# Empty slices in the projection schedule of a stick-breaking attention layer, a later split of the turned values, and a lead-in stepped at every second slot

## The chip, the cores and the metric

The kernel runs on one core of a Trainium2 chip. A core has a matmul engine (TensorE, PE in the profile; its weight loads are PEld), three engines for elementwise work (VectorE or DVE, ScalarE or ACT, GpSimd or POOL) and SyncE (SP), which here issues the DMAs. Each engine works through its own list of instructions in order, and semaphores make one wait for another. Matmul results land in PSUM, which has eight banks of 128 x 512 numbers; everything else lies in SBUF or in device memory.

The metric is the time of one execution on the device, in microseconds (us): the median over several.

## The reference

One layer of a transformer with 2048 tokens of width 1024: a norm, stick-breaking attention with 16 heads of 64, an output projection with residual, another norm, and a gated feed-forward part (width 2816). The part that matters here, for each block of 128 queries (h is the normed and modulated input):

```python
qkv = (h @ w_qkv).reshape(b, s, 3, N_HEADS, HEAD_DIM)
z = jnp.einsum('bthd,bshd->bhts', q[:, q0:end], k[:, :end]).astype(jnp.float32) * scale
mask = s_pos < t_pos
sp = jnp.where(mask, jax.nn.softplus(z), 0.0)
rest = lax.cumsum(sp, axis=3, reverse=True)
log_a = jnp.where(mask, z - rest, -jnp.inf)
a = jnp.exp(log_a).astype(v.dtype)
outs.append(jnp.einsum('bhts,bshd->bthd', a, v[:, :end]))
...
return o @ w_o
```

The kernel uses that a weight is sigmoid(z) times the product of sigmoid(-z) over the later keys, so each row needs two sigmoids, one running product (a scan) and one multiplication.

## The kernel before

All matrix products are made from numbers split in a high and a low half: high times high, high times low, low times high. Each operand therefore needs a split first, a copy that rounds (ScalarE) and a subtraction (VectorE or GpSimd).

**Units and slots.** Heads are handled in 8 pairs, tokens in 4 blocks of 512. A unit is one head, one block of queries and one block of keys; there are 160. A unit takes four slots, one for each 128 queries, so the attention stage has 640 slots, and the loop at lines 1067 to 1099 writes out, slot by slot, what each engine is to do: the scheduler is switched off for the four compute engines (line 165), and what is written first runs first on its engine. SP isn't among them; its DMAs are ordered by the framework.

A slot runs stages of several units at once (`ORDER_IN_SLOT`, lines 57 to 61). Of slot s: `score` (two matmuls into `z`), `sigmoids` (ScalarE twice), `break_sticks` (the scan on VectorE, then a multiplication on GpSimd); of the weights made six slots before: `turn` (four 128 x 128 transposes into a PSUM tile `t`, two turns in every even slot), `split_high` (ScalarE's copy) and `split_low` (VectorE's subtraction) into `aT`; of nine slots before: `weigh_values` (two matmuls into the accumulator `o`). In even slots the turns stand behind the projection and ahead of the sigmoids and splits.

**Projections between.** Between `score` and `turn` stands `proj`: a part of the projections of queries, keys and values, which are computed block by block as the attention goes on (`project`, lines 376 to 483). For each of 32 steps (a head pair and a token block) it makes three products, keys, queries, values, each in 8 slices of three matmuls (`mm3`), into a tile `pj`. Behind the keys and behind the queries `split` copies the result out of PSUM, and DMAs move it to its place. The values are copied to `vT`; `VGAP` = 2 empty slices later `values_turn` transposes them into PSUM (`vt`, four transposes) and splits them (lines 463 to 476). `project` is a generator: each `yield` ends a slice, and `project_to` (line 500) advances it to a given count of slices. `SLICES` says how many slices each step has, `AHEAD` how many must be done at the start, and `RATE` spreads the rest evenly over the slots (a slot on the diagonal counts 0.8). The first two steps are done differently (`early`): their values are turned within the next steps.

**PSUM.** Three pools hold the eight banks: `zps` 3 (`z`), `tps` 2 (`t`), `accps` 3. The last is shared by `pj`, `vt`, `o`, some of the turned inputs `xT`, and the sums `ap` of the modulation, which other generators (`late`, line 1073) put between the slots.

**The end of the stage.** When all slices are done, at slot 608, `first_out`, the output projection of the first token block, is begun; from 28 slots before the end of the units on it makes one slice in each slot. Its inputs, the attention's outputs, are loaded, added (GpSimd) and split by `lead_in` (lines 967 to 976), inputs 6 and 7 by a second call of it. That generator is stepped from line 1077 in every third slot and from line 1087.

The rest of the kernel (output projection, norm, feed-forward) is the same before and after.

Of the kernel before, what the change touches and what calls it, by code (L numbers as in the profile page):

```python
# [19 lines left out]
KC = D // P  # L20
NH = 16
HD = 64
NPAIR = NH // 2
BT = 512
NB = S // BT
# [11 lines left out]

VGAP = 2

SLICES = [0, 3 * KC] + [3 * KC + VGAP] * (NPAIR * NB - 2)  # L40


AHEAD = 6 * KC + 6
DIAG_WEIGHT = 0.8
RATE = (sum(SLICES) - AHEAD) / (NPAIR * (48 + 32 * DIAG_WEIGHT) - 24 - 8 * DIAG_WEIGHT)

# [40 lines left out]
def hybrid_trunk_kernel(  # L87
# [83 lines left out]
    def sb(shape, dtype, **kw):  # L171

        return (odd if kw["tag"] in ODD_TAGS else att).tile(shape, dtype, **kw)
# [5 lines left out]
    def load_weights(p, t, tag="wraw"):  # L179
        raw = sb([P, KC, P], F32, name=f"wr{p}_{t}", tag=tag, bufs=BUFS[tag])  # L180
        nc.sync.dma_start(raw, wqkv[p, t])
        raws[p, t] = raw
# [152 lines left out]
    def h_load(p, b):  # L335
        h = []
        for k2 in range(KC // 2):
            ht = sb([P, 2, 2, BT], F32R, name=f"ht{p}_{b}_{k2}", tag="ht", bufs=BUFS["ht"])
            nc.sync.dma_start(f32(ht), h_s[b][:, 2 * k2 : 2 * k2 + 2])
            h += [ht[:, 0], ht[:, 1]]  # L340
        return h
# [14 lines left out]
    waiting = []  # L356
# [19 lines left out]
    def project(at):  # L376

        p, b = STEPS[at]
        begun = (p, b) == (0, 0)
        early, parked = (p, b) in EARLY, (p, b) == PARKED  # L380

        nb = STEPS[at + 1][1] if at + 1 < len(STEPS) and STEPS[at + 1][0] == 0 else None
        if STEPS[at] == (PARKED[0], 1):
            unpark()
        h = norm_h[b] if p == 0 or parked else h_load(p, b)

        def product(t):
            if begun:
                return first_acc[t]
            w = weights[p, t]  # L390
            if parked and t == 1:
                acc = zps.tile([P, BT], F32, name=f"pj{p}_{b}_{t}", tag="z")
            else:
                acc = accps.tile([P, BT], F32, name=f"pj{p}_{b}_{t}", tag="acc")
            ahead = b == NB - 1 and p + 1 < NPAIR
            for k in range(KC):
                if t == 1:
                    if p == 0:
                        first_norm(b, k + 3)
                    if k == 0 and nb and nb > 1:  # L400
                        x_load(nb)
                    if k == 5 and waiting:
                        waiting.pop()()
                if parked and t == 1 and k % 2 == 0:
                    nc.sync.dma_start(*stores[k // 2])
                if parked and (t, k) == (1, 6):
                    split_early(1, 2, ["whl"])
                if t == 0 and nb:
                    (x_square if k < 4 else x_scale)(nb, k % 4)
                if t == 2 and k in (2, 4, 6):  # L410
                    first_norm(nb, k // 2 - 1)
                if ahead and k == 0:
                    load_weights(p + 1, t)
                if ahead and k == 6:
                    split_weights(p + 1, t)
                mm3(acc, (w[0][:, k], w[1][:, k]), (h[k][:, 0], h[k][:, 1]), k == 0, k == KC - 1)
                yield
            return acc

        def split(acc, tag):  # L420
            hl = sb([P, 2, BT], F32R, name=f"{tag}n{p}_{b}", tag="qkn", bufs=BUFS["qkn"])
            nc.scalar.copy(hl[:, 0], acc)
            nc.vector.tensor_tensor(hl[:, 1], acc, f32(hl[:, 0]), op=ALU.subtract)
            return hl

        closing = (p, b) == (NPAIR - 1, NB - 1)
        if closing:
            wo_load(0, 0, "whl")
            wo_load(0, 1, "ht")
        n = split((yield from product(1)), "k")  # L430
        if closing:
            wo_load(0, 2, "whl")
        if parked:
            nc.sync.dma_start(k_park, f32(n))
        else:
            kt = sb([P, 2, BT], F32R, name=f"kt{p}_{b}", tag="kt", bufs=BUFS["kt"])
            for e in range(2):
                for part in range(2):
                    nc.sync.dma_start(
                        f32(kt[part * HD : (part + 1) * HD, e]), f32(n[e * HD : (e + 1) * HD, part])  # L440
                    )
            keys[p, b] = kt

        n = split((yield from product(0)), "q")
        if closing:
            wo_load(0, 3, "whl")
        if parked:
            nc.sync.dma_start(q_park, f32(n))
        else:
            qt = sb([P, 2, 2, BT], F32R, name=f"qt{p}_{b}", tag="qt", bufs=BUFS["qt"])  # L450
            for e in range(2):
                for half in range(2):
                    nc.sync.dma_start(
                        f32(qt[half * HD : (half + 1) * HD, e]), f32(n[e * HD : (e + 1) * HD])
                    )
            queries[p, b] = qt

        acc = yield from product(2)
        tag = "w" if early else "tmp"
        vT = sb([P, BT], F32, name=f"vT{p}_{b}", tag=tag, bufs=BUFS[tag])  # L460
        nc.scalar.copy(vT, acc)

        def values_turn():
            pool, ptag = (zps, "z") if early else (accps, "acc")
            pt = pool.tile([P, 4, 2, HD], F32, name=f"vt{p}_{b}", tag=ptag)
            for i in range(4):
                nc.tensor.transpose(
                    pt[:, i].rearrange("p e d -> p (e d)"), vT[:, i * P : (i + 1) * P], ident
                )
            v = sb([P, 4, 2, 2, HD], F32R, name=f"v{p}_{b}", tag="v", bufs=BUFS["v"])  # L470
            nc.scalar.copy(v[:, :, :, 0], pt)
            nc.vector.tensor_tensor(v[:, :, :, 1], pt, f32(v[:, :, :, 0]), op=ALU.subtract)
            if parked:
                nc.sync.dma_start(v_park, f32(v))
            else:
                values[p, b] = v

        if early:
            waiting.append(values_turn)
            return  # L480
        for _ in range(VGAP):
            yield
        values_turn()

    units = [
        (p, e, qb, sc)
        for p in range(NPAIR)
        for qb in range(NB)
        for e in range(2)
        for sc in range(qb, -1, -1)  # L490
    ]
# [8 lines left out]
    def project_to(n):  # L500

        nonlocal done
        while done < min(n, sum(SLICES)):
            next(pending)
            done += 1
        if done == sum(SLICES):
            next(pending, None)
# [557 lines left out]
    first_out = None  # L1065
    project_to(AHEAD - EAGER)
    for s in range(4 * len(units) + last):
        if s % 4 == 0 and s // 4 < len(units):
            p, e, qb, sc = units[s // 4]
            at = STEPS.index((p, qb)) if (p, qb) != PARKED else STEPS.index((p, 1)) - 1  # L1070
            project_to(sum(SLICES[: at + 1]) + 1)
        if s >= LATE_FROM and s % LATE_STEP == 0:
            next(late, None)
        if s >= SPLIT_FROM and s % SPLIT_STEP == 0:
            next(wo_weights, None)
        if s >= lead_from and s % WO_STEP == 0:
            next(ahead_of_wo, None)
        if done == sum(SLICES):
            if first_out is None:
                first_out = out_projection(0)  # L1080
                for k2, tag in enumerate(("ht", "ht", "ht", "ht")):
                    wo_load(1, k2, tag)
                for step in ahead_of_wo:
                    pass
                ahead_of_wo = lead_in(6, KC)
            elif s < 4 * len(units):
                next(ahead_of_wo, None)
            if s == 4 * len(units):
                gate_load(0, gate)
            if s >= 4 * len(units) - OUT_BEFORE:  # L1090
                for _ in range(1 if s < 4 * len(units) else 3):
                    next(first_out, None)
        for stage, delay in ORDER_IN_SLOT[s % 2]:
            if stage == "proj":
                i = min(s // 4, len(units) - 1)
                weight += DIAG_WEIGHT if units[i][2] == units[i][3] else 1.0
                project_to(AHEAD - max(0, EAGER - 1 - s) + weight * RATE)
            elif 0 <= s - delay < 4 * len(units):
                stages[stage](*divmod(s - delay, 4))
# [501 lines left out]
```

## Time and profile before

| | us |
|---|---|
| median of three runs | 2847.78 |
| lowest and highest | 2846.89, 2852.01 |
| the profiled execution | 2847.31 |
| its span, from the first to the last instruction of the program | 2845.1 |

In the profile, "busy" is the time in which an engine has an instruction running; `x` gives a number of instructions. A row of waits names the engine that stood still, the line and the tile of the instruction that couldn't start, and what it waited for, then the total, the number of waits and the longest. A row of the timeline has the start and the length in us, engine, line, operation, output and inputs, shape, and in brackets how long the engine was idle before and what ended that. Matmuls are pipelined: one of 512 columns is shown with some 0.39 us, but the next starts after 0.23 us; starts tell the pace. The attention stage lies between about 50 and 1390 us.

### The profile page before, as it was taken

To read this page: it belongs to the slowest core of one execution; us is meant where nothing else is said; L and a number is where in the kernel's file an instruction comes from. 1 tells how busy PE (TensorE), PEld (TensorE's weight loads), DVE (VectorE), ACT (ScalarE), POOL (GpSimd) and SP (SyncE) were. 2 spreads that over 40 slices of the span, in tenths; PEclk is the share of its full clock that TensorE was granted. 3 is DMA by queue.
4 is the path that set the end of the run, shared out by engine and by line. 5 is a ranking of instruction groups with operands and counts; after the bars stand their busy time and mean duration, and the time that the engine had idled before them with its cause. 6 is when DMAs were issued, how large, how long until landed. Compare 5 with 4: busy or idle time off the path is not lost.

```text
span 2845.1 us, 41790 instructions
## 1 busy us (share of the span) xinstructions
PE 2795.6 (98%) x13848; PEld 2333.9 (82%) x13848; DVE 2028.4 (71%) x2822; ACT 1632.3 (57%) x3265; POOL 1277.0 (45%) x2032
## 2 busy tenths in 40 slices
PE   7999999999999999999999999999999999999998
PEld 6788888888888888887888888888788888888887
DVE  6788898888888888888866766555775665133467
ACT  5787877788787877777645533333433333322243
POOL 1475666676576655656410122221222222544454
PEclk9999999999999999999999999999999999999999
DMA  8765556656665635546289645435453335545566
GB/s 329 271 211 167 189 155 227 211 170 234 189 209 192 209 118 179 196 133 231 88 299 312 203 137 152 122 98 161 130 177 108 112 107 163 191 142 155 180 214 195
DMA packets 239368, 516.84 MB, mean 182 GB/s; under 512 B 22321, under 2 KB 110385, under 8 KB 221489
## 3 DMA queue, kind: packets, MB, share of 16 engines
q1 hardware_dynamic: 239152, 514.18, 56.0%
q8 instruction: 109, 1.79, 0.3%
q14 instruction: 107, 0.87, 0.1%
HBM read 346.85 MB, written 118.49 MB: 164 GB/s over the span
## 4 chain that ended last, share of the span: by engine, by line
PE 87%; DVE 6%; ACT 2%; DMA 2%; issue 2%; POOL 1%; SPq 0%; DVEq 0%; POOLq 0%; ACTq 0%
PE s L155 9%; PE s L156 9%; PE s L157 9%; PE z L519 8%; PE o L598 8%; PE t L570 8%; PE pj L155 6%; PE pj L156 6%; PE pj L157 6%; PE o L156 4%; PE o L157 4%; PE o L155 4%; PE y L157 2%; PE y L155 2%; PE y L156 2%
## 5 line engine op out<-in xcount | busy, mean ns | idle before, releaser
L560 POOL TENSOR_TENSOR a<-a,w 128x512 f32<-128x512 f32 (+3 forms) x640 | 619.4, 968 | 217.8 <-DVE w L553 126.8
L553 DVE TENSOR_TENSOR_SCAN w<-z,c,begin 128x512 f32<-128x512 f32 x384 | 489.6, 1279 | 81.2 <-ACT z L538 61.5
L155 PE MATMUL s<-r,l 128*128 128x512 f32 x1232 | 481.4, 391 | 4.3 <-DVE p L1364 3.7
L157 PE MATMUL s<-r,l 128*128 128x512 f32 x1232 | 479.4, 389 | 0.0
L156 PE MATMUL s<-r,l 128*128 128x512 f32 x1232 | 479.3, 389 | 0.0
L536 ACT ACTIVATE a<-z 128x512 f32<-128x512 f32 (+3 forms) x640 | 347.2, 543 | 167.2 <-PE z L519 135.7
L598 PE MATMUL o<-aT,v 128*128 128x512 f32 (+3 forms) x1280 | 384.3, 381 | 0.1
L586 DVE TENSOR_TENSOR aT<-t,aT 128x512 fp32r<-128x512 f32 (+3 forms) x640 | 359.3, 596 | 22.9 <-ACT aT L580 22.2
L519 PE MATMUL z<-kt,qt 128*128 128x512 f32 (+3 forms) x1280 | 363.1, 365 | 0.0
L580 ACT CAST aT<-t 128x512 fp32r<-128x512 f32 (+3 forms) x640 | 314.1, 533 | 73.5 <-PE t L570 63.5
L538 ACT ACTIVATE z<-z 128x512 f32<-128x512 f32 (+3 forms) x640 | 344.8, 539 | 0.0
L1372 POOL TENSOR_TENSOR one<-p,p 128x512 f32<-128x512 f32 x44 | 70.5, 1602 | 577.8 <-issue 320.5
L155 PE MATMUL pj<-ht,w 128*128 128x512 f32 x768 | 309.7, 403 | 7.6 <-ACT ht L705 2.6
L156 PE MATMUL pj<-ht,w 128*128 128x512 f32 x768 | 302.0, 393 | 1.2 <-DVE ht L710 0.7
L570 PE MATMUL t<-begin,a 128*128 128x128 f32 x2176 | 294.8, 273 | 8.5 <-DVE aT L586 7.2
L570 PEld LDWEIGHTS t<-begin,a 128*128 128x128 f32 x2176 | 255.1, 140 | 58.0 <-DVE aT L586 10.8
L157 PE MATMUL pj<-ht,w 128*128 128x512 f32 x768 | 302.1, 393 | 0.0
L155 PEld LDWEIGHTS s<-r,l 128*128 128x128 f32 x1232 | 231.3, 188 | 54.4 <-ACT l L1225 2.9
L157 PEld LDWEIGHTS s<-r,l 128*128 128x128 f32 x1232 | 231.3, 188 | 48.2
L156 PEld LDWEIGHTS s<-r,l 128*128 128x128 f32 x1232 | 231.3, 188 | 47.9 <-issue 0.5
L548 DVE TENSOR_TENSOR_SCAN w<-z,begin 128x128 f32<-128x128 f32 (+3 forms) x256 | 208.8, 818 | 75.0 <-ACT z L538 62.2
L519 PEld LDWEIGHTS z<-kt,qt 128*128 128x128 f32 x1280 | 230.3, 188 | 37.4 <-DVE w L548 0.2
(160 smaller groups left out, 4865.8 us busy)
## 6 DMA issues: line engine op xcount, KB each, us to landing
ht<-h_s SPq DMA_DIRECT2D x108, 1024.0 KB, 8.1
wi<-in_win SPq DMA_DIRECT2D x86, 512.0 KB, 4.0
qt<-qn SPq DMA_DIRECT2D x124, 256.0 KB, 4.8
ol_qt<-act_s SPq DMA_DIRECT2D x56, 512.0 KB, 3.7
act_s<-S SPq DMA_DIRECT2D x66, 256.0 KB, 4.1
br<-in_wout SPq DMA_DIRECT2D x66, 256.0 KB, 3.6
h_s<-ht SPq DMA_DIRECT2D x16, 1024.0 KB, 7.8
o_s<-os SPq DMA_DIRECT2D x128, 128.0 KB, 2.4
```

Source lines behind the costliest of these rows:

```text
L155: nc.tensor.matmul(acc, lhs[0], rhs[0], start=first, stop=False, **kw)
L156: nc.tensor.matmul(acc, lhs[0], rhs[1], start=False, stop=False, **kw)
L157: nc.tensor.matmul(acc, lhs[1], rhs[0], start=False, stop=last, **kw)
L519: nc.tensor.matmul(z[:, :n], q[:, e, part, r * P : (r + 1) * P], k[:, e, :n], start=part == 0, stop=part == 1,)
L536: nc.scalar.activation(a[:, :n], z[:, :n], AF.Sigmoid, scale=QK_SCALE)
L538: nc.scalar.activation(z[:, :n], z[:, :n], AF.Sigmoid, scale=-QK_SCALE)
L553: nc.vector.tensor_tensor_scan(rest[:, rev], left[:, rev], begin[:, :BT][:, rev], initial=carries[r], op0=ALU.mult, op1=ALU.bypass,)
L560: nc.gpsimd.tensor_tensor(a[:, :n], a[:, :n], rest[:, 1 : n + 1], op=ALU.mult)
L570: nc.tensor.transpose(pt[:, rb * P : (rb + 1) * P], weighed[i, rb][:, j * P : (j + 1) * P], ident)
L580: nc.scalar.copy(hl[:, 0, t0:], pt[:, t0:])
L586: nc.vector.tensor_tensor(hl[:, 1, t0:], pt[:, t0:], f32(hl[:, 0, t0:]), op=ALU.subtract)
L598: nc.tensor.matmul(acc[:, t0:], lhs, hl[:, part, t0:], start=sc == qb and j == 0 and part == 0, stop=sc == 0 and j == 3 and part == 1,)
```

## The change

A step of the projections now has four more slices: an empty one behind the split of the keys, one behind that of the queries, one between the transposes of the values and their split, and one behind that split. The counts (`SLICES`, `AHEAD`, and `RATE` from them) follow. The two early steps keep their slices. In the end of the stage, the second call of `lead_in` is stepped in even slots where it was stepped in every one. No instruction is added, removed or reshaped.

```diff
 VGAP = 2
-SLICES = [0, 3 * KC] + [3 * KC + VGAP] * (NPAIR * NB - 2)
-AHEAD = 6 * KC + 6
+PAUSES = 4
+SLICES = [0, 3 * KC] + [3 * KC + VGAP + PAUSES] * (NPAIR * NB - 2)
+AHEAD = 6 * KC + 6 + PAUSES
...
         n = split((yield from product(1)), "k")
+        if not early:
+            yield
...
         n = split((yield from product(0)), "q")
+        if not early:
+            yield
...
                 nc.tensor.transpose(
                     pt[:, i].rearrange("p e d -> p (e d)"), vT[:, i * P : (i + 1) * P], ident
                 )
+            return pt
+
+        def values_split(pt):
             v = sb([P, 4, 2, 2, HD], F32R, name=f"v{p}_{b}", tag="v", bufs=BUFS["v"])
             nc.scalar.copy(v[:, :, :, 0], pt)
             nc.vector.tensor_tensor(v[:, :, :, 1], pt, f32(v[:, :, :, 0]), op=ALU.subtract)
...
         if early:
-            waiting.append(values_turn)
+            waiting.append(lambda: values_split(values_turn()))
             return
         for _ in range(VGAP):
             yield
-        values_turn()
+        pt = values_turn()
+        yield
+        values_split(pt)
+        yield
...
-            elif s < 4 * len(units):
+            elif s < 4 * len(units) and s % 2 == 0:
                 next(ahead_of_wo, None)
```

## The prediction

> **What bounds the kernel now.** I read the page first, then busy time by stretch, then who waited for whom, then groups by shape, then the timeline around the longest waits. The page:
>
> ```profile
> span 2845.1 us, 41790 instructions
> PE 2795.6 (98%) x13848; PEld 2333.9 (82%) x13848; DVE 2028.4 (71%) x2822; ACT 1632.3 (57%) x3265; POOL 1277.0 (45%) x2032
> PEclk9999999999999999999999999999999999999999
> ht<-h_s SPq DMA_DIRECT2D x108, 1024.0 KB, 8.1
> ```
>
> PE is busy for 98% of the span at the full clock, so PE's order of work matters only where PE waits. The edit adds, removes and reshapes no instruction; it can move at most the 49.5 us in which PE is idle, or lengthen them. The edit acts in the attention stage. Busy time by stretch (PE, PEld, DVE, ACT, POOL, then clock and DMA):
>
> ```profile
> 200.00:1300.00 1100.00, 1089.93 (x6011) 924.27 (x6010) 943.24 (x1225) 865.54 (x1826) 697.00 (x1450) 1.00 0.58 186
> 1326.00:1336.00 10.00, 8.57 (x56) 7.16 (x56) 8.90 (x12) 7.79 (x18) 6.22 (x14) 1.00 0.97 396
> ```
>
> From 200 to 1300 us PE idles 10.07 us, and VectorE is busy for 86%: not the bound over the stage, but near enough to become it wherever PE's load per slot drops. The second row is such a place already (the last block's projections are over, the output projection not yet begun): PE drops to 86% there, VectorE rises to 89%. The same stretch for the score matmuls alone (PE, PEld) counts the slots, two matmuls each:
>
> ```profile
> 200.00:1300.00 1100.00, 308.08 (x1086) 195.52 (x1086) 1.00 0.58 186
> ```
>
> 1086 / 2 = 543 slots, 2.03 us each. What PE waited for, from 200 to 1300, then from 60 to 200 (three rows), then from 1300 to 1360 (the last row); columns are total, times, longest:
>
> ```profile
> PE t L570 <- DVE aT L586: 3.3, 7, 0.8
> PE pj L155 <- issue: 1.4, 1, 1.4
> PE pj L155 <- DVE qn L423: 1.4, 1, 1.4
> PE pj L155 <- DVE kn L423: 0.9, 1, 0.9
> PE ap L277 <- DVE v L472: 0.7, 1, 0.7
> PE vt L467 <- ACT vT L461: 0.7, 1, 0.7
> PE t L570 <- POOL w L188: 0.6, 1, 0.6
> ...
> PE xT L315 <- DVE qn L423: 1.0, 1, 1.0
> PE t L570 <- DVE aT L586: 1.0, 3, 0.5
> PE pj L155 <- ACT hf L325: 0.9, 1, 0.9
> ...
> PE t L570 <- DVE aT L586: 2.9, 4, 1.2
> ```
>
> Two kinds of wait. A transpose `t` waits for a PSUM buffer that `split_low` on VectorE has not emptied: VectorE is late. A product `pj` (or `xT`) waits for an `accps` buffer that the splits of keys or queries, or a neighbour, still hold: there are three, and PE asks for the next at once.
>
> **The change part by part.**
>
> *Empty slice behind keys and queries.* Now the next product's first matmul stands in the same slice as the split of the one before. Timeline rows of the longest such wait:
>
> ```profile
> 545.55 0.39 PE L157 MATMUL pj<-ht,w 128*128 128x512 f32 x1
> 545.98 0.59 ACT L422 CAST qn<-pj 128x512 fp32r<-128x512 f32 x1 [1.77 <-PE pj L157]
> 546.60 0.69 DVE L423 TENSOR_TENSOR qn<-pj,qn 128x512 fp32r<-128x512 f32 x1 [0.91 <-ACT qn L422]
> 547.35 0.50 PE L155 MATMUL pj<-ht,w 128*128 128x512 f32 x1 [1.40 <-DVE qn L423]
> ```
>
> PE ends the queries at 545.94, ScalarE and VectorE need until 547.29, and PE stands. With an empty slice PE first does a slot's values and scores. Starts of neighbouring 512-wide matmuls, and one pair of turns:
>
> ```profile
> 299.46 1.04 PE L570 MATMUL t<-begin,a 128*128 128x128 f32 x8
> ...
> 301.48 0.39 PE L156 MATMUL pj<-ht,w 128*128 128x512 f32 x1
> 301.71 0.39 PE L157 MATMUL pj<-ht,w 128*128 128x512 f32 x1
> ```
>
> 0.23 us a matmul, so two of values and two of scores are 0.92 us, a slice of projection (three) 0.69 us, and eight transposes, in every second slot, at most 1.04 us: an empty slot is at most 0.92 + 0.52 = 1.44 us of PE work. The empty slice thus covers 0.92 us of a wait: the 0.9 us (`kn`) goes wholly, the 1.4 us (`qn`) leaves 0.5. That is -1.8. The same for `xT<-qn`, before 200 us: -0.9. Bounds: 0, if another buffer is late next (`o`, `ap`, `vt` share the ring), and -3.3, if all three go.
>
> *Empty slice behind the values, split a slice later.* The wait put down to issue is the same kind: VectorE's modulation work before the values' split held the buffer.
>
> ```profile
> 863.89 0.17 DVE L239 SCALAR_TENSOR_TENSOR g_eff<-sc,gc 128x4 f32<-128x4 f32 x1
> 863.96 0.47 PE L155 MATMUL pj<-ht,w 128*128 128x512 f32 x1 [1.42 <-issue]
> ```
>
> The next block's first product now comes one or two slots after the four transposes of the values instead of right behind them: -0.9 of 1.4 (bounds 0 and -1.4). `ap<-v` (0.7) stays: that split isn't earlier. ScalarE no longer meets the transposes still running. VGAP stays 2 slices but slices pass faster, so the transposes may meet ScalarE's copy `vT` a little sooner: 0.7 us once now, once more is 0 to +0.7; I take 0.
>
> *Slices pass faster.* 804 slices become 924 and AHEAD goes from 54 to 58; worked through RATE's own line, 1.34 becomes 1.55 slices for each full slot, about 0.14 us more PE work in a slot between pauses. In the order in which the two built programs' instructions stand, slots 12 to 603 without a projection matmul go from 43 to 96: a block's end had one or two, followed by a slot with the values' transposes and a product; now it has two or three, the transposes among them, and single ones stand behind keys and queries.
>
> *The price.* ScalarE and VectorE work of a full slot, by shape, 200 to 1300 us (busy, mean ns, then idle before):
>
> ```profile
> L553 DVE TENSOR_TENSOR_SCAN w<-z,c,begin 128x512 f32<-128x512 f32 x325 | 414.3, 1279 | 71.5 <-ACT z L538 54.5 <-POOL c L559 6.2 <-POOL w L535 4.0
> L586 DVE TENSOR_TENSOR aT<-t,aT 128x512 fp32r<-128x512 f32 x379 | 244.2, 675 | 10.8 <-ACT aT L580 10.6
> L536 ACT ACTIVATE a<-z 128x512 f32<-128x512 f32 x380 | 230.8, 607 | 97.2 <-PE z L519 83.3 <-POOL a L560 4.4 <-POOL w L535 4.1
> L538 ACT ACTIVATE z<-z 128x512 f32<-128x512 f32 x380 | 229.2, 603 | 0.0
> L580 ACT CAST aT<-t 128x512 fp32r<-128x512 f32 x379 | 211.8, 595 | 48.5 <-PE t L570 47.8
> L472 DVE TENSOR_TENSOR v<-vt,v 128x512 fp32r<-128x512 f32 x26 | 17.6, 677 | 2.7 <-ACT v L471 2.5
> L471 ACT CAST v<-vt 128x512 fp32r<-128x512 f32 x26 | 15.8, 609 | 6.7 <-PE vt L467 6.7
> ```
>
> VectorE needs 1.28 + 0.68 = 1.95 us a slot, ScalarE 1.81, an empty slot of PE 1.44: each falls VectorE 0.5 us behind, and `v` adds 0.68. How this comes to a stop is seen at one block's end (PE, timeline):
>
> ```profile
> 302.84 0.60 PE L570 MATMUL t<-begin,a 128*128 128x128 f32 x4
> 303.99 0.31 PEld L570 LDWEIGHTS t<-begin,a 128*128 128x128 f32 x3 [0.78 <-DVE aT L586]
> ```
>
> Second turn of a pair: it waits for the buffer before last. Bounds of one more empty slot at 29 ends: 0, if the slack covers it all (3.3 us over some 27 ends now is 0.12 each, so most ends have slack to spare), and 29 x 0.5 = +14.5 if none does. I take half of what these waits cost now, +1.7, nearer the lower end: the slots between the pauses carry 0.14 us more each, which lets VectorE catch up, and the 6.7 us for which ScalarE stood before `v` on unfinished transposes go from the chain turn, copy, subtract. Behind keys and queries only one slot is empty, with slack restored: bounds 0 and 58 x 0.5 = +29; I take +0.5, next to the lower one, because slots with one and two slices stand directly on both sides.
>
> *First block's last outputs.* `lead_in(6, KC)` has five steps: load of 6, load of 7, add of 6, add of 7 with the split of 6, split of 7. Two places call it: line 1077 in every third slot, which stays, and line 1087, now in every slot, then in even ones. From slot 608, where both programs see the last slice done, that gives now 609 (both loads), 610, 611, 612, and then 609, 610, 612 (both adds and the split of 6) and 614: the order of POOL's instructions shows the two adds side by side. The split on ScalarE comes right behind its own add instead of a slot later. Already now it has to wait:
>
> ```profile
> 1336.78 0.62 ACT L941 CAST ohl<-of 128x512 fp32r<-128x512 f32 x1 [1.64 <-POOL w L533]
> 1338.94 0.66 PE L570 MATMUL t<-begin,a 128*128 128x128 f32 x4 [1.19 <-DVE aT L586]
> ```
>
> ScalarE stood 1.64 us for POOL, the turned weights' copies behind it in its queue, VectorE's `ohl` subtract behind that, and PE 1.19 us for the subtract after it. With the distance of one slot (2.03 us) gone ScalarE stands up to that much longer; against it, from slot 612 on PE has 0.69 us of output projection in each slot, so it comes later to the turn that waits. Bounds -1.2 (the later place heals it) and +2.0; I take +1.5, nearer the upper one, since POOL's queue in front of the add (multiply 1.1 us, copy) is the same. The halves of 6 are used at slot 618, of 7 at 619, five or six slots behind their splits. The stretch without projections there is one slot longer: +0.5 (0 to +0.5).
>
> *Queues.* SP's order shifts by a place or two of small transfers; POOL's weight splits move by at most a slot. A tile of `ht` lands in 8.1 us (first fence); between its last read and its next lie 10 slices before, 12 now, over 7 slots or some 15 us. Cost nothing; if that cover went, a late tile would cost what 8.1 us exceeds.
>
> *Sum.* -1.8 - 0.9 - 0.9 + 1.5 + 1.7 + 0.5 + 0.5 = +0.6 us. The profiled execution took 2847.31 (span 2845.1 and 2.2 around it), 0.5 under the median of the three runs, 2847.78. 2847.3 + 0.6 = 2847.9: no change.
>
> **The rivals.** 0.2% is 5.7 us, about what a measurement here can tell from no change.
>
> *VectorE becomes the bound at block ends (slower).* Place: the second turn of a pair after the values. For: 1.95 against 1.44 us, and the 8.90 of 10 us in the stretch without projections. Against: most ends have slack. Gains (-3.6) against 14.5 at the ends, a quarter of the 29 behind keys and queries (7) and 2.0 for the lead-in and its longer stretch is +20: 2867; half of the first two gives +9, 2856. Without any price behind keys and queries it decides from 0.25 us an end (29 x 0.25 = 7.3 = 5.7 + 3.6 - 2.0).
>
> *The gaps heal too (faster).* ScalarE no longer stands before `v`, the slices between the pauses are denser, and `t<-aT` goes as well: of the 10.07 us in the stage all but the two 0.7 and the 0.6 (8.1), 2.8 before 200 and 2.9 at the end is -13.8: 2833.5; half is 2840.5.
>
> *Nothing moves but places.* Each wait reappears at another buffer, only the lead-in's 2.0 is added: 2849.3.
>
> *The clock drops.* By the row at 1326, ten microseconds almost without projections ran at 1.00, so the empty slots shouldn't lose it; if one did, 29 gaps of two slots at 1.44 us would double: +84, 2931. [...]
>
> **How the numbers follow.** Forecast, terms that nearly cancel, with "nothing but places" inside the band of no change: 0.50. Gaps heal: 0.26. VectorE bound: 0.23. Clock: 0.01. The range takes the half-effects and a little more, 2838 to 2858; outside are the full rivals and the clock, under 2 in 10. The likeliest case's own range is 2842 to 2853. Faster by over 0.2%: 0.26; within: 0.50; slower: 0.24.
>
> **What would show it.** Right: `pj<-kn`, `pj<-qn`, `xT<-qn` and the 1.4 us of issue gone or under 0.5; ScalarE's idle before `v` near zero; ScalarE before the first `ohl` of 6 idle for over 1.64 us and PE's wait behind it longer than 1.19; `t<-aT` between 3 and 7 us from 200 to 1300. Wrong: `t<-aT` over 10 us (slower), or near zero (faster); a `pj` or `o` that waits for a new holder of `accps`; PEclk under 1.

## The result, and the profile after

The changed kernel takes 2862.56 us (median; 2859.12 to 2868.31) against 2847.98 for the kernel before (2846.89 to 2852.01): ratio 1.0048, 95% interval 1.0038 to 1.0058 (ratios here and below are estimated over all the runs, so they can differ a little from the quotient of the medians, here 1.0051). It is slower by some 14.6 us, where no change was forecast. The profiled execution took 2862.93 us.

The page's lines, then busy time by stretch (PE, PEld, DVE, ACT, POOL, clock, DMA), of the changed kernel:

```profile
span 2861.1 us, 41812 instructions
PE 2804.8 (98%) x13848; PEld 2338.5 (82%) x13848; DVE 2021.7 (71%) x2822; ACT 1627.8 (57%) x3265; POOL 1275.0 (45%) x2032
```

```profile
200.00:1300.00 1100.00, 1085.41 (x5972) 917.50 (x5971) 930.70 (x1216) 853.60 (x1810) 688.22 (x1436) 1.00 0.57 183
```

Each of the five rows of engines has the same number of instructions as before (the page's total of all kinds is 41812, it was 41790). The span is 16.0 us longer. From 200 to 1300 PE idles 14.6 us, it was 10.1, and the window holds 39 matmuls fewer. What PE waited for, from 200 to 1300:

```profile
PE t L582 <- DVE aT L598: 9.3, 22, 0.7
PE pj L157 <- DVE qn L425: 1.8, 2, 1.0
PE pj L157 <- ACT os L616: 1.1, 1, 1.1
PE vt L473 <- ACT vT L467: 0.7, 1, 0.7
PE pj L157 <- DVE kn L425: 0.4, 1, 0.4
PE t L582 <- POOL c L571: 0.4, 1, 0.4
PE pj L157 <- DVE gr L282: 0.2, 1, 0.2
PE t L582 <- POOL a L572: 0.2, 1, 0.2
```

The transposes' waits for VectorE's subtraction went from 3.3 us in 7 places to 9.3 in 22. Their mechanism at one block's end (timeline, rows of PE and VectorE, ScalarE's copies into `aT` and its `v` copy):

```profile
520.80 2.46 DVE L565 TENSOR_TENSOR_SCAN w<-z,c,begin 128x512 f32<-128x512 f32 x2 [0.77 <-ACT z L550]
...
521.29 0.60 PE L473 MATMUL vt<-begin,vT 128*128 128x128 f32 x4
...
521.59 0.62 ACT L592 CAST aT<-t 128x512 fp32r<-128x512 f32 x1
...
522.07 0.63 ACT L480 CAST v<-vt 128x512 fp32r<-128x512 f32 x1
...
522.54 0.64 ACT L592 CAST aT<-t 128x512 fp32r<-128x512 f32 x1
...
523.18 0.67 DVE L598 TENSOR_TENSOR aT<-t,aT 128x512 fp32r<-128x512 f32 x1
...
523.76 0.68 DVE L481 TENSOR_TENSOR v<-vt,v 128x512 fp32r<-128x512 f32 x1
...
523.90 0.66 PE L582 MATMUL t<-begin,a 128*128 128x128 f32 x4 [0.57 <-DVE aT L598]
...
524.36 0.68 DVE L598 TENSOR_TENSOR aT<-t,aT 128x512 fp32r<-128x512 f32 x1
...
525.18 0.63 PE L582 MATMUL t<-begin,a 128*128 128x128 f32 x4 [0.63 <-DVE aT L598]
```

PE has run through slots without a product, so two scans stand in VectorE's queue back to back, then a subtraction, the values' subtraction, another subtraction, with no gap between them. ScalarE's copies for the two subtractions had ended 0.97 and 1.18 us before these began. PE reaches the turns and stands 0.57 us for the first buffer and 0.63 for the second.

A row of waits counts only the gaps that the profile gives to one releaser, and its matmuls overlap: those shown with 0.39 us start 0.23 us apart. The trace's starts tell more. I take the start of each slot's first score matmul as the slot's mark, and call a matmul late by its start-to-start distance from the one before it less the median distance of the same pair of kinds in the kernel before, where that is over 0.06 us. Between the marks of slots 40 and 600 this gives, for the kernel before and after: length 1136.0 and 1143.4 us; transposes `t` late by 7.7 us in 24 places and 15.9 in 42; `pj` late by 7.7 and 4.9. Of the transposes' 7.7 us, 5.7 lie within 6 us behind the values' copy `vT`, at 11 of the stage's 26 block ends; after, 11.0 at 19 of 26. Within 6 us behind the copies of keys and queries lay 0.6, now 2.7.

The starts also show what the late turns waited for. In the changed kernel the first transpose of a turn is late in 40 places between the two marks, 15.4 us in all. Each of them starts 0.05 to 0.15 us after VectorE has ended the subtraction of two turns before, which frees its buffer. In 37 of them (14.4 us) that subtraction had begun over 0.15 us after ScalarE's copy for it was finished, in the median of the 40 places 0.8 us: VectorE was busy with other work all that time. It hadn't always been kept busy before: in some two thirds of the 37 it stood idle for part of the 3 us ahead (0.5 us in the mean of all), as for 0.77 us in the first row above, where it waited for ScalarE's sigmoid. So ScalarE has a part in VectorE's lateness; how large it is wasn't tested.

At the lead-in (timeline, then PE's waits from 1300 to 1370):

```profile
1354.12 0.62 ACT L953 CAST ohl<-of 128x512 fp32r<-128x512 f32 x1 [3.90 <-POOL of L946]
...
1357.79 1.73 PE L582 MATMUL t<-begin,a 128*128 128x128 f32 x7 [3.09 <-DVE aT L598]
```

```profile
PE t L582 <- DVE aT L598: 4.8, 3, 3.1
```

ScalarE waits 3.90 us ahead of the first split of input 6, 1.64 before, and PE 3.09 behind it, 1.19 before.

The changed kernel reaches the mark of slot 639 16.1 us later. This splits into 4.3 up to slot 40, 7.4 from 40 to 600, and 4.4 from 600 on, all by the two profiled executions.

### The profile page after: what moved, and what is told of

Its sections match the earlier page's. It is cut to its first block, busy times and chain, and to the rows that moved or that the text cites. A ratio compares the mean times of both kernels' runs of the same rounds, so it can differ in the third digit from the quotient of the medians.

```text
span 2861.1 us, 41812 instructions
## 1 busy us (share of the span) xinstructions
PE 2804.8 (98%) x13848; PEld 2338.5 (82%) x13848; DVE 2021.7 (71%) x2822; ACT 1627.8 (57%) x3265; POOL 1275.0 (45%) x2032
## 4 chain that ended last, share of the span: by engine, by line
PE 83%; DVE 6%; ACT 3%; DMA 3%; issue 3%; POOL 2%; SPq 0%; DVEq 0%; POOLq 0%; ACTq 0%
PE s L157 9%; PE s L159 9%; PE s L158 9%; PE z L531 8%; PE o L610 8%; PE t L582 7%; PE pj L157 5%; PE pj L158 5%; PE pj L159 5%; PE o L159 4%; PE o L158 4%; PE o L157 4%; PE y L159 1%; PE y L157 1%; PE y L158 1%
```

## The experiments

The theory after the result (A): in consecutive slots without a product PE outruns VectorE, whose subtractions release the transposes' buffers; the lead-in's loss is the missing slot between GpSimd's add and its split. Rivals: the pauses behind keys and queries do it (58 of them), the start does it, or ScalarE and the latency of the chain do it, whatever VectorE needs.

**The lead-in alone.**

```diff
-            elif s < 4 * len(units):
+            elif s < 4 * len(units) and s % 2 == 0:
```

> Only the lead-in at even slots, no pauses. Theory A (POOL's two adds and the first split now stand in one slot, so ScalarE waits about 4 us for POOL and PE about 3 us): 3 to 5 us over the kernel before, one wait of PE t for aT of 2.5 to 3.5 us near 1340 to 1350 us, the first 1300 us unchanged, and perhaps a clock window at half there. Theory B (the wait belongs to the longer stretch without projections that the pauses make): within 1 us of before, longest such wait near the 1.2 us of before.

Measured 2852.1 us against 2849.03, ratio 1.0007 [0.9998, 1.0015]. Waits of PE from 1300 to 1420, and the timeline of the split of input 6:

```profile
PE t L570 <- DVE aT L586: 4.5, 3, 3.1
```

```profile
1344.34 2.53 POOL L934 TENSOR_TENSOR of<-op 128x512 f32<-128x512 f32 x2
1345.67 0.62 ACT L941 CAST ohl<-of 128x512 fp32r<-128x512 f32 x1 [3.90 <-POOL of L934]
1346.32 1.10 DVE L942 TENSOR_TENSOR ohl<-of,ohl 128x512 fp32r<-128x512 f32 x1 [3.23 <-ACT ohl L941]
...
1349.34 1.06 PE L570 MATMUL t<-begin,a 128*128 128x128 f32 x7 [3.09 <-DVE aT L586]
```

The two adds lie side by side on GpSimd, ScalarE stands 3.90 us for the first (1.64 before), VectorE 3.23 behind it, PE 3.09 (1.19 before). From slot 600 to 639 the stage takes 79.4 us, before 77.7: +1.7. The rows are as expected, and the clock stays at full speed there (1.00 from 1340 to 1350 and from 1350 to 1360 us). The price in this stretch is smaller than the 3 to 5 us expected, and the interval of the ratio includes 1.

**All pauses, the lead-in as before.**

```diff
+PAUSES = 4
+SLICES = [0, 3 * KC] + [3 * KC + VGAP + PAUSES] * (NPAIR * NB - 2)
...
-            elif s < 4 * len(units) and s % 2 == 0:
+            elif s < 4 * len(units):
```

> All four pauses, lead-in as before the change. Theory A (three separate costs: start, block ends and pauses, lead-in): 9 to 12 us over before, with slot 600 some 11 us late as in the whole change, and nothing added after slot 612. Theory B (lead-in harmless): as the whole change, about 14.5 us over before, with the 3 us wait still there.

2859.65 against 2849.03, ratio 1.0033 [1.0021, 1.0045]; slots 40 to 600 take 1143.5 us, slots 600 to 639 take 78.4. Most of the loss belongs to the pauses, the rest to the lead-in. The stretch from slot 600 contains an interval at half clock here (0.50 from 1343.76 to 1347.17 us; see the last section).

**Only behind keys and queries.**

```diff
+PAUSES = 2
...
         n = split((yield from product(1)), "k")
+        if not early:
+            yield
...
         n = split((yield from product(0)), "q")
+        if not early:
+            yield
```

> Pauses behind keys and queries only. My prediction's terms: the waits of pj for kn and qn shrink, 1 to 3 us faster than before. Rival (the single empty slots cost VectorE its slack as the block ends do): 3 to 6 us slower, with t waiting for aT behind keys and queries.

2850.79 against 2849.03, ratio 1.0004 [0.9995, 1.0012]. Slots 40 to 600: 1137.6 us, +1.6, between the two expectations: neither the forecast gain nor the rival's 3 to 6 us. PE's waits from 200 to 1300:

```profile
PE t L579 <- DVE aT L595: 5.6, 12, 0.8
```

**Only around the values' split.**

```diff
+PAUSES = 2
...
-        values_turn()
+        pt = values_turn()
+        yield
+        values_split(pt)
+        yield
```

> Only the two slices around the values' split. Theory A (the block ends carry the cost of the pauses): 5 to 9 us slower than before, t waiting for aT over 6 us in total from 200 to 1300 us against 3.3. Rival (the keys' and queries' pauses carry it): within 2 us of before, t for aT under 4 us.

2862.54 against 2849.03, ratio 1.0048 [1.0036, 1.006]: as slow as the whole change. Slots 40 to 600: 1148.4 us, +12.4, more than the 5 to 9 us expected. The same row:

```profile
PE t L578 <- DVE aT L594: 11.0, 23, 0.9
```

The pauses behind the values carry the loss. Added to them, those behind keys and queries take 5.0 us off this stage (1148.4 to 1143.4), though alone they add 1.6; by lateness 1.2 of it are transposes and 0.8 products, the rest isn't accounted for.

**Two slots between the lead-in's add and split, in the kernel before.**

```diff
-        for n in range(first, end + 3):
+        for n in range(first, end + lag):
...
-            if first <= n - 3 < end:
-                o_prep(0, n - 3)
+            if first <= n - lag < end:
+                o_prep(0, n - lag)
...
-                ahead_of_wo = lead_in(6, KC)
+                ahead_of_wo = lead_in(6, KC, 6)
```

> Kernel before with the lead-in's splits of inputs 6 and 7 three steps later than the adds' neighbours, so two slots lie between POOL's add and ScalarE's split. If ScalarE's wait for POOL is what delays PE there: that wait falls from 1.6 us to under 0.5, PE's 1.2 us behind it goes, 1 to 2 us between slots 608 and 620. If the stretch without projections sets it: nothing changes there.

2847.78 against 2848.34, ratio 0.9999 [0.999, 1.0008]. The stretch from slot 600 takes 76.1 us, 1.6 less than before, with this row left from 1300 to 1420:

```profile
PE t L570 <- DVE aT L586: 1.4, 2, 0.8
```

The distance between add and split is what this wait hangs on, in both directions; its price is some 1.6 us, too small for the whole time to show. ScalarE no longer waits ahead of the split of input 6, where it waited 1.64 us.

**No pauses in the first head pair.**

```diff
-SLICES = [0, 3 * KC] + [3 * KC + VGAP] * (NPAIR * NB - 2)
+PAUSES = 4
+SLICES = [0, 3 * KC] + [3 * KC + VGAP + (PAUSES if p else 0) for p, b in STEPS[2:]]
...
         n = split((yield from product(1)), "k")
+        if p and not early:
+            yield
```

> The four pauses from the second head pair on, the first pair's three steps as before, lead-in as before. If the 3 us that slots 20 to 40 lost belong to the pauses in the first pair (where the norm's work stands beside them): slots 20 to 40 as before, and 2 to 4 us less than with all pauses. If they are chance of the start: no difference from all pauses.

2862.71 against 2848.96, ratio 1.0051 [1.0039, 1.0063]. A miss: slots 20 to 40 took 41.9 us before, 45.1 after, and 46.1 here, where no pause stands in them and only slices pass faster. So the pauses in the first pair aren't what the start loses by.

**Values split a slice after their transposes, no slice added.**

```diff
-        for _ in range(VGAP):
+        for _ in range(VGAP - 1):
             yield
-        values_turn()
+        pt = values_turn()
+        yield
+        values_split(pt)
```

> Kernel before with the values' split a slice behind their transposes, but no slice added: the transposes move one slice earlier (one empty slice ahead of them in place of two). Theory A (it is the number of slots without projection at a block's end that costs): slot 40 to 600 within 2 us of before. Rival (the later split itself costs, because it falls among the next turn's splits): 4 us or more over before, t for aT over 6 us.

2848.91 against 2848.34, ratio 1.0 [0.9991, 1.0009]; transposes late by 4.8 us instead of 7.7, `vt` by 2.9 instead of 0.8. Without an added slice, the split's later place costs nothing.

**No empty slices at all.**

```diff
-VGAP = 2
+VGAP = 0
+TURN_AT = 2
...
-                    if k == 5 and waiting:
+                    if k == (5 if at == 2 else TURN_AT) and waiting:
                         waiting.pop()()
...
-        for _ in range(VGAP):
-            yield
-        values_turn()
+        waiting.append(values_turn)
```

(The last step has two slices more, in which it turns its own values.)

> Kernel before with no empty slice at all at block ends: the values are turned and split inside the next block's keys (third slice). Theory A (VectorE falls behind in slots without projection): t for aT from 200 to 1300 us falls from 3.3 us to under 1.5, and the stage loses 2 to 6 us unless a third holder of accps makes pj wait. Rival (the split of the values in the way, wherever it stands): t for aT stays at 3 us or more.

2845.72 against 2848.34, ratio 0.9987 [0.9978, 0.9996]: a little faster. Slots 40 to 600: 1133.7 us, -2.3; PE's waits of a transpose for VectorE are 2.2 us, not under 1.5 as expected; transposes late by 3.4 us in 9 places, products by 11.3 (7.7 before). PE's waits and ScalarE's group of the `v` copies, 200 to 1300:

```profile
PE t L574 <- DVE aT L590: 2.2, 5, 0.6
```

```profile
L473 ACT CAST v<-vt 128x512 fp32r<-128x512 f32 x26 | 15.3, 587 | 22.8 <-PE vt L469 22.8
```

ScalarE stood 6.7 us for the transposes ahead of this copy in the kernel before; here 22.8 us, in a kernel that is quicker. So this wait of ScalarE isn't what sets the time.

**The four extra empty slices spread inside the products.**

```diff
+PAUSES = 4
+PAUSE_AT = {(1, 3), (0, 3), (2, 2), (2, 5)}
...
+                if not early and (t, k) in PAUSE_AT:
+                    yield
```

> Kernel before with four more empty slices in a step, but inside the products (behind the 4th slice of keys and queries, the 3rd and 6th of the values), so the pace between is the same 1.55 a slot as in the change, while the block ends keep their two slices. Theory A (empties in a row at the block end cost): within 3 us of before. Rival (the faster pace and uneven slots cost by themselves): 6 us or more over before.

2851.32 against 2848.34, ratio 1.0008 [1.0, 1.0017]; slots 40 to 600 +1.9 us. As many empty slices as the change adds, a quarter of its loss in this stage.

**One empty slice behind the values' split.**

```diff
+PAUSES = 1
...
         values_turn()
+        yield
```

> One more empty slice, behind the values' split. Theory A (cost by the number of empty slots in a row): 2 to 5 us over before from slot 40 to 600, between before (0) and the two slices around the split (12). Rival (only the slice between transposes and split costs): under 1 us.

2857.47 against 2848.96, ratio 1.0031 [1.002, 1.0043]; slots 40 to 600 +8.0 us, over the 2 to 5 expected; transposes late by 12.6 us.

**Four empty slices ahead of the values' transposes.**

```diff
-VGAP = 2
+VGAP = 4
...
-AHEAD = 6 * KC + 6
+AHEAD = 6 * KC + 8
```

> Two more empty slices, both ahead of the transposes of the values (VGAP 4), split in the same slice as they. Theory A (the number in a row decides, not the place): 6 us or more over before, near the kernel with the two slices around the split. Rival (the place of the split decides): under 3 us.

2867.15 against 2848.96, ratio 1.0067 [1.0054, 1.008]; slots 40 to 600 +15.9 us. Among the kernels without slices behind keys and queries the order is by empty slices in a row at a block's end: 0, 2, 3 and 4 of them cost -2.3, 0, +8.0 and +12.4 or +15.9 us there. The changed kernel doesn't fit in: it has 4 in a row and costs 7.4, less than 3 alone. So the number in a row isn't the whole of it.

**No empty slices, and two slots between add and split.**

```diff
+TURN_AT = 2
...
+                ahead_of_wo = lead_in(6, KC, 6)
```

> No empty slice at block ends and the splits of inputs 6 and 7 later: both found gains together. If they add: 3 to 5 us under before (the first alone 2.6, the second alone 1.6 in its stretch). If the second was chance: 2 to 3 us.

2845.65 against 2848.96, ratio 0.999 [0.9982, 0.9998]. Both stretches keep their gains in the profile (slots 40 to 600 -2.4 us, from 600 to 639 -2.3), whose page shows

```profile
span 2841.8 us, 41800 instructions
```

3.3 us less than the kernel before. The whole time is no shorter than without empty slices alone (ratio 0.9987), so it doesn't show the second gain. These two are the only kernels with the full work whose interval lies below the kernel before.

**VectorE's subtraction cut short, in three kernels.** The low half of the product of weights and values is left out. PE's work and order stay, and the subtraction that releases the transposes' buffers goes from 0.68 to 0.21 us (group of the kernel before with the edit, 200 to 1300):

```profile
L586 DVE TENSOR_TENSOR aT<-t,aT 128x64 fp32r<-128x64 f32 x546 | 103.0, 210 | 32.6 <-ACT aT L580 28.3
```

This tests whether VectorE's time is what the transposes wait for. It doesn't tell VectorE's backlog from the latency of the chain transpose, copy, subtraction, since the subtraction is a link of that chain and gets 0.47 us shorter in it. The backlog is seen in the starts above: in 37 of 40 late turns VectorE began its subtraction late. The edit also frees the second matmul of the values from waiting for VectorE. That matters little, for these matmuls are late by 1.5 and 1.8 us with the whole subtraction (kernel before, changed kernel) and by 1.6 and 1.8 with the short one.

```diff
-            hl[:, 1, t0:], pt[:, t0:], f32(hl[:, 0, t0:]), op=ALU.subtract
+            hl[:, 1, t0 : t0 + 64], pt[:, t0 : t0 + 64], f32(hl[:, 0, t0 : t0 + 64]), op=ALU.subtract
...
-                acc[:, t0:], lhs, hl[:, part, t0:],
+                acc[:, t0:], lhs, hl[:, 0, t0:],
```

In the kernel before:

> The kernel before, with VectorE's subtraction on the turned weights (0.68 us for 512 columns) cut to 64 columns, and the second matmul of the values reading the high half again, so that TensorE's work stays the same; the low half of the product of weights and values is left out. VectorE loses some 0.5 us a slot. Theory (VectorE's backlog in empty slots stops TensorE): the waits of a transpose for aT go to under 1 us from 200 to 1300, and slots 40 to 600 get 2 to 6 us shorter than in the kernel before (its transposes' excess is 7.7 us there). Rival (the chain transpose, ScalarE's copy, release, whatever VectorE does): 3 us of such waits stay, and the length is as before within 2 us.

In the changed kernel:

> The changed kernel with the same thin subtraction; the low half of the product of weights and values is left out. Theory: its slots 40 to 600 are within 2 us of the kernel before with the thin subtraction, because VectorE no longer falls behind however many slots are empty in a row; the waits for aT at block ends go to under 2 us, and what is left of the loss (2 to 8 us) lies in the first 40 slots and behind slot 600. Rival (ScalarE's copies or PE's order itself): at least 5 us over the thin kernel before in slots 40 to 600.

With four empty slices ahead of the transposes:

> Four empty slices ahead of the values' transposes (the costliest placing, +15.9 us in slots 40 to 600) with the same thin subtraction; the low half of the product of weights and values is left out. Theory: within 3 us of the thin kernel before in slots 40 to 600. Rival: at least 10 us over it.

They took 2839.4, 2846.92 and 2853.18 us against 2848.98, ratios 0.9965 [0.9952, 0.9978], 0.999 [0.9981, 1.0] and 1.0017 [1.0008, 1.0027]. In the first of them 1.4 us of the transposes' waits stay, where under 1 was expected, and its stage is 6.5 us shorter, just over the 2 to 6. Busy times from 200 to 1300 in the second of them (VectorE, third, 754 us instead of 931), and PE's waits there:

```profile
200.00:1300.00 1100.00, 1092.61 (x6032) 928.49 (x6031) 754.23 (x1230) 864.20 (x1835) 700.60 (x1456) 1.00 0.58 187
```

```profile
PE t L582 <- DVE aT L598: 1.8, 7, 0.5
PE pj L157 <- DVE qn L425: 1.7, 2, 1.0
PE pj L157 <- issue: 1.6, 1, 1.6
```

| slots 40 to 600, us | whole subtraction | short subtraction |
|---|---|---|
| kernel before | 1136.0 | 1129.5 |
| changed kernel | 1143.4 (+7.4) | 1130.8 (+1.3) |
| four empty slices ahead | 1151.9 (+15.9) | 1141.5 (+12.0) |

For the change the theory holds: with VectorE's subtraction short, its 7.4 us in this stage shrink to 1.3 and the transposes' waits to 1.8 us, with all its empty slots in place. With four empty slices ahead of the transposes it falls: 12.0 of 15.9 us stay. There the transposes still wait 4.2 us for VectorE, and the rows name other releasers beside it, the scan among them:

```profile
PE t L570 <- DVE aT L586: 4.2, 9, 0.7
PE pj L155 <- DVE qn L423: 1.7, 2, 1.0
PE pj L155 <- issue: 1.6, 1, 1.6
PE z L519 <- DVE w L553: 1.5, 3, 0.7
```

By lateness transposes have 7.6 us there, scores `z` 4.2 and products 10.2, where the kernel before with the short subtraction has 2.3, 0.1 and 7.8. So something else costs there as well. The length of the gap alone can't be it, since the changed kernel has four empty slices in a row too. What differs is that all four stand ahead of the values' transposes, and that no slice stands behind keys and queries. Which of these it is, or whether ScalarE's 1.81 us a slot against PE's 1.44 plays a part, wasn't tried.

The short subtraction takes away only this stage's part of the loss: by the medians the changed kernel is still 7.5 us behind the kernel before, both with it, where it was 14.6. In the profiles, slots 20 to 40 take 44.0 us against 41.7, and the stretch from slot 600 to 639 79.5 against 76.8, with ScalarE still waiting 3.91 us for GpSimd's adds. Another 4.2 us lie behind slot 639, where the work is the same; over all the profiled kernels that stretch scatters from 1452.7 to 1457.0 us.

## Why the prediction was wrong

**The step that failed** is "I take half of what these waits cost now, +1.7, nearer the lower end", for the block ends. Transposes became late by 5.3 us more within 6 us of the values' copy, and the waits in the rows grew by 6.0. With the slices around the values' split alone the stage grew by 12.4 us, 0.48 for each of its 26 ends. The mechanism was in the text as the first rival (0.5 us that VectorE falls behind in an empty slot), which decides from 0.25 us an end by the prediction's own sum. In the whole change the transposes' lateness that doesn't lie behind keys and queries grew by 6.1 us, 0.23 an end. The 2867 of its full form and the 2856 of the half one enclose the 2862.9 of the profiled execution.

By stretch, the terms against the profile: up to slot 40 -0.9 forecast and +4.3 measured, from 40 to 600 -0.5 (-2.7 + 1.7 + 0.5) and +7.4, from 600 to 639 +2.0 and +4.4. So the stage with the block ends holds the largest miss, 7.9 us; the start holds 5.2 and the stretch from 600 on 2.4.

**What misled it** was "most ends have slack". That came from the 7 waits of the row `t<-aT`. By starts 11 of 26 ends already paid, 5.7 us: at these the slack was used up before the change. The second reason, denser slots that let VectorE catch up, was no match for two more empty slices. The third, the 6.7 us for which ScalarE stood before `v`, was worth nothing: they went (1.6 now), as forecast, and the kernel without empty slices has 22.8 and is quicker.

**Behind keys and queries**, +0.5: lateness went from 0.6 to 2.7 us, +2.1, within its bounds and nearer the lower one, but four times the value taken.

**The gains** were -1.8, -0.9 and -0.9. In rows 200 to 1300 the waits answer one to one: `pj<-qn` 1.4 became 0.98 at 551.81, `kn` 0.87 became 0.37, the 1.42 put down to issue became 1.06 for `os`, and a new `qn` of 0.87 stands at 768.25. They came to less than half. At 551.81 VectorE's part of the split begins 0.79 us after ScalarE's has ended, with a scan between them; before the change it began 0.03 us after. So the empty slot delays the split too. By starts products are late by 2.8 us less, near the 2.7 forecast for the stage: the sum came out while the parts it was made of didn't, which is luck. `xT<-qn` (1.0) is gone; in its place two waits of a transpose for GpSimd's `w` stand in the changed kernel (its waits from 60 to 200, first rows):

```profile
PE xT L317 <- DVE xn L308: 1.8, 5, 0.4
PE t L582 <- POOL w L545: 1.8, 2, 1.5
PE t L582 <- DVE aT L598: 1.5, 2, 0.9
```

**The lead-in** was costed +1.5 and measured +1.7 alone. In the whole change the stretch from 600 is 82.2 us against 78.4 without the lead-in's part: +3.8; there PE's idle 3.09 us is followed by an interval at half clock (0.50 from 1357.59 to 1361.01 us; below). The extra slot without a product, +0.5, isn't shown: the pauses alone add 0.7 there (78.4 against 77.7), but with an interval at half clock (0.50 from 1343.76 us on), and the kernel with the values' slices alone takes 77.4.

**The clock rival** was given 84 us and a chance of 0.01. That 29 gaps run at half clock, as the 84 us take, no run shows. By the windows there are three intervals of 3.41 us at 0.50 in the changed kernel, from 87.83, 1343.94 and 1357.59 us on, at most an estimated 1.7 us each (last section), none at the block ends (the clock is 0.50 at the very end of the program as well, from 2856.04 us on, and in the kernel before from 2839.57 on, where PE has no work left): so it was rightly held unlikely, but a few short intervals lie between nothing and the 84 us. The queues cost nothing, as said: no row of a wait of PE for a DMA appears in the attention stage (50 to 1390 us).

**The start** (3.2 us from slot 20 to 40) was in no term. It stays open. It isn't the pauses in the first pair, and VectorE's subtraction explains at most 0.9 of it (2.3 us stay with the short one). Chance has a part in what comes before: kernels with the same instructions up to slot 20 reach it at times up to 5.0 us apart.

## What to carry to other kernels

Price a schedule's empty slots by the engine that is nearly full, and by how many stand in a row: here 2, 3 and 4 empty slices in a row cost 0, +8 and +7 to +16 us, and four more spread out +2. Where they stand matters as much: the +7 has further ones behind keys and queries, the +16 has all four ahead of the values' transposes, and why these differ is open. Read the slack from starts against the usual distance, before trusting a row of waits: 3.3 us in 7 waits were 7.7 us in 24 places. Between a producer on one engine and a consumer in another engine's in-order queue leave the slot that the producer's own queue needs: the wait on the add cost 1.7 us when the slot was taken away, and gave back 1.6 when two were put between.

## What the runs showed of the hardware

In the changed kernel's attention stage the half clock comes in intervals of 3.41 us, each behind an interval in which PE was idle for much of the time (1.45 us or more). Windows of the changed kernel (PE first, then PEld, DVE, ACT, POOL, clock), for two of the three the half-clocked interval and the one ahead of it:

```profile
1340.53:1343.94 3.41, 1.71 (x14) 1.28 (x13) 3.41 (x5) 2.98 (x8) 2.44 (x4) 1.00 1.00 423
1343.94:1347.35 3.41, 3.41 (x13) 2.93 (x12) 2.87 (x5) 1.48 (x4) 1.87 (x7) 0.50 1.00 408
1354.18:1357.59 3.41, 0.52 (x3) 0.10 (x1) 2.82 (x4) 3.41 (x7) 2.20 (x4) 1.00 0.00 0
1357.59:1361.01 3.42, 3.22 (x11) 2.88 (x12) 3.42 (x5) 2.52 (x6) 2.40 (x4) 0.50 0.00 0
```

PE was busy for 1.71 and 0.52 of the 3.41 us ahead (ahead of the third, from 87.83 us on, for 1.96). The distances between these three are whole multiples of 3.413 us (1343.94 less 91.25 is 367 of them, 1357.59 less 1343.94 is 4). Thin work alone doesn't decide it. In the kernel with only the lead-in's edit PE stands for 3.09 us as well, up to 1349.34 us; 3.41 us that hold the end of this gap have 1.48 us of work, and the next kept the full clock:

```profile
1347.41:1350.82 3.41, 1.48 (x10) 1.31 (x11) 3.41 (x5) 3.41 (x8) 1.40 (x4) 1.00 0.00 0
1350.82:1354.24 3.42, 3.39 (x17) 2.50 (x16) 3.42 (x6) 2.98 (x7) 3.09 (x6) 1.00 0.01 2
```

What decides stays open. In the interval from 87.83 us on, products of 512 columns start 0.42 to 0.43 us apart (88.45, 88.88, 89.30 us), right behind it 0.23 (91.31, 91.54, 91.77 us). So an interval at half clock costs at most about half of its 3.41 us, an estimated 1.7 us. The mean granted clock of the profiled execution was 0.999 in the kernel before, 0.997 in the changed kernel and from 0.997 to 0.999 in the others. Whether half-clocked intervals are part of why the whole times scatter by a few us, beside what the stage shows, was not shown.
